# Attention heads: a copy moved from ScalarE to VectorE, low parts to GpSimd, reciprocals of softmax sums taken in pairs

## The chip, the cores and the metric

The kernel runs on one core of one Trainium2 chip. The metric is device time of one execution in microseconds (us); lower is better. Engines are named as in the profile: PE is TensorE (PEld its weight loads), ACT is ScalarE, DVE is VectorE, POOL is GpSimd, SP the queue that issues most DMAs.

## The reference

A two-layer encoder trunk over two independent sequences of 512 tokens, width 1024, in float32: Fourier mixing and an MLP, then attention and an MLP. The change lies in the attention layer: 8 query heads, 2 key/value heads, head size 128.

```python
s = jnp.einsum("bqkgd,bskd->bkgqs", q_blk, k)
p = jax.nn.softmax(s, axis=-1)
o = jnp.einsum("bkgqs,bskd->bqkgd", p.astype(v.dtype), v)
...
return o @ w_o
```

`x_prompt` is sequence 0 and `x_sample` sequence 1; both use the same weights.

## The kernel before, in words

TensorE multiplies in float32r, which holds fewer bits than float32. So nearly every operand is kept as two parts: `hi`, the rounded value (a ScalarE cast, line 86), and `lo`, what is left of it (a VectorE subtraction `src - hi`, line 87). Both stand in the helper `split`. A product is three matmuls: hi by hi, hi by lo, lo by hi (`mm3`, lines 81 to 83). Matmul results lie in PSUM, in tiles `ps` of 128 by 512, of which there are eight.

Attention runs over 16 heads, eight of sequence 0 and then eight of sequence 1. One turn n of the loop handles three heads at once:

1. `scores` for head n, four times, t = 0 to 3 (128 queries each): three matmuls; VectorE takes the row maximum (line 1385); ScalarE the exponential with its row sum (line 1387, tile `p`); VectorE the reciprocal of the sum (line 1388); GpSimd multiplies `p` by it in place (line 1389).
2. `transpose_p` for head n-1, four times, mixed with the scores: four TensorE transposes, one from each of the four finished `p` tiles (line 1395), into one `ps`, then `split` into the operand of step 4. So every group of four transposes reads all four `p` of its head, the last one `p` of t = 3.
3. `transpose_q` for head n+1: four transposes (line 1374) and a `split`.
4. `values` for head n-1: twelve matmuls into one `ps`, `o`. ScalarE copies `o` to SBUF as float32 (line 1412); for sequence 0 alone `split` also makes hi and lo parts from it, which the output projection after the loop reads first (the products `b11` and `b21`, line 820).

In turns 3 to 7 the normalisation of the last query tiles (`norm_rope`, with a square root, lines 136 and 1340 to 1353) runs as a side job, and from turn 7 on the loop also loads and splits projection weights (`load_kept`, tiles `w`), in every second turn. The tiles `p` come from a pool of eight.

In this loop a scheduler puts the instructions of every engine in order, from estimated costs. Every engine then runs its queue strictly in that order, waiting at semaphores.

Of the kernel before, what the change touches and what calls it, by code (L numbers as in the profile page):

```python
# [15 lines left out]
AF = mybir.ActivationFunctionType  # L16
ALU = mybir.AluOpType
# [27 lines left out]
def trunk_kernel(ctx, tc, x_in, xt_in, y_out, tables, rope, gfour, gcol, grow, gfin,  # L45
                 w_four, w_nyq, w_qkv, w_o, w_a22, w_up, w_row2, w_row4, w_sum2, w_sum4, w_down):
    nc = tc.nc
# [13 lines left out]
    def nm(s):  # L61
        n_[0] += 1
        return f"{s}_{n_[0]}"

    def slot(shape, dt):
        return act.tile(shape, dt, tag="u4", name=nm("u"))

    def tm(shape=(P, 512), dt=F32):
        return tmp.tile(list(shape), dt, tag="t2", name=nm("t"))

    def small(n=4):
        return sm.tile([P, n], F32, tag="s", name=nm("s"), padded_shape=[P, 8])

    def ps():
        return psp.tile([P, 512], F32, tag="ps", name=nm("ps"))

    def f32(ap):
        return ap.bitcast(F32)

    def mm3(out, lh, ll, rh, rl, first, last):  # L80
        nc.tensor.matmul(out, lh, rh, start=first, stop=False)  # L81
        nc.tensor.matmul(out, lh, rl, start=False, stop=False)  # L82
        nc.tensor.matmul(out, ll, rh, start=False, stop=last)  # L83

    def split(dst_hi, dst_lo, src, eng=nc.vector):
        nc.scalar.copy(dst_hi, src)  # L86
        eng.tensor_sub(dst_lo, src, f32(dst_hi))  # L87
# [502 lines left out]
    def odd_outs(q, fos):  # L590
        return outs(q, fos, wo, 256, 256)
# [28 lines left out]
    with tc.manual_schedule(engines={ET.PE, ET.Activation, ET.DVE, ET.Pool, ET.SP}):  # L620
# [72 lines left out]
        o = odd_outs(0, range(KC))  # L693
# [596 lines left out]
    for which, sc in (("q", HD ** -0.5), ("k", 1.0)):  # L1290
        r = slot([P, 2, NT, HD], F32)
# [7 lines left out]
    def qkv(cg, q, t, ws, k0=0, k1=KC, o=None):  # L1299
        o = ps() if o is None else o  # L1300
        cols = slice(t * P, (t + 1) * P)
        for k in range(k0, k1):
            w = ws[k // 2]
            c = (k % 2) * 512
            mm3(o, hT[q][k][:, 0, cols], hT[q][k][:, 1, cols],
                w[0][:, c : c + 512], w[1][:, c : c + 512], k == 0, k == KC - 1)
        return o
# [50 lines left out]
    heads_out, ahead = Blocks(None), []  # L1358
# [11 lines left out]
    def transpose_q(q, h):  # L1370
# [5 lines left out]
        split(qT[:, 0], qT[:, 1], pt)  # L1376
        return qT

    def scores(q, h, qT, t):
        kk = kT[q, h // 4]  # L1380
        s = ps()
        cols = slice(t * P, (t + 1) * P)
        mm3(s, qT[:, 0, cols], qT[:, 1, cols], kk[:, 0], kk[:, 1], True, True)
        m, sm_ = small(1), small(1)
        nc.vector.tensor_reduce(m[:, :1], s, AX.X, ALU.max, negate=True)
        p = tm()
        nc.scalar.activation(p, s, AF.Exp, bias=m[:, :1], accum_out=sm_[:, :1])  # L1387
        nc.vector.reciprocal(sm_[:, :1], sm_[:, :1])
        nc.gpsimd.tensor_scalar(p, p, sm_[:, :1], 1.0, ALU.mult, ALU.mult)
        return p  # L1390

    def transpose_p(probs, sc):
# [7 lines left out]
    def values(q, h, pts):  # L1400
        o = ps()
        c = (h // 4) * HD
        for sc in range(NT):
            vh, vl = vt[q][0][:, sc, c : c + HD], vt[q][1][:, sc, c : c + HD]
            mm3(o, vh, vl, pts[sc][:, 0], pts[sc][:, 1], sc == 0, sc == NT - 1)
        i, j = h // 2, h % 2
        name = "b11" if h < 4 else "b21"
        if j == 0:
            heads_out.f[q, i] = slot([P, 2, 512], F32)
            if q == 0:  # L1410
                heads_out.b.setdefault(name, []).append([slot([P, 2, 512], F32R) for _ in range(2)])
        nc.scalar.copy(heads_out.f[q, i][:, j], o)
        if q == 0:
            hi, lo = heads_out.b[name][-1]
            split(hi[:, j], lo[:, j], o)

# [142 lines left out]
    with tc.manual_schedule(engines={ET.Activation}):  # L1561
        o = qkv(1, 1, 2, ws[1])
        probs = [scores(*heads[0], first, t) for t in range(NT)]
        nc.scalar.activation(raw[:, :512], o, AF.Copy, scale=rs[1][:, 2:3])
        qT = transpose_q(*heads[1])
        for _ in turned:
            pass
        o = qkv(1, 1, 3, ws[1])
        nc.scalar.activation(raw[:, 512:], o, AF.Copy, scale=rs[1][:, 3:4])
        head_squares(raw, 0, 4, ss)  # L1570
# [4 lines left out]
    for n in range(1, len(heads) + 1):  # L1575
        pts, nxt = [], []
        for t in range(NT):
            if n < len(heads):
                nxt.append(scores(*heads[n], qT, t))
            pts.append(transpose_p(probs, t))  # L1580
            if n > 2 and t == 0:
                for _ in range(3 if n == 3 else 1):
                    next(todo, None)
        last = nxt[-1] if nxt else last
        if n + 1 < len(heads):
            qT = transpose_q(*heads[n + 1])
        values(*heads[n - 1], pts)
        if n == 2:
            head_squares(raw, 4, 4, ss)
        probs = nxt  # L1590
        if n > 6:
            next(first_rows, None)
# [18 lines left out]
    with tc.manual_schedule(engines={ET.PE}):  # L1611
        o = {}
# [12 lines left out]
        o = {}  # L1625
# [24 lines left out]
        o = {}  # L1650
# [22 lines left out]
    for f in range(2 * PLAIN):  # L1673
        raw = load_raw(plain[f], (P, 2, 512))
        hi, lo = slot([P, 2, 512], F32R), slot([P, 2, 512], F32R)
# [59 lines left out]
    with tc.manual_schedule(engines={ET.PE, ET.Activation, ET.DVE, ET.Pool, ET.SP}):  # L1735
# [17 lines left out]
        x, z = xtok  # L1753
# [3 lines left out]
        def tile(t, c0, c1, at=0, mid=lambda: None):  # L1757
            o = ps()[:, : c1 - c0]
            for k in range(len(ats)):
                ak, wk = ats[k][1], ws[k]  # L1760
                cols = slice(t * P, (t + 1) * P)
                mm3(o, ak[0][:, cols], ak[1][:, cols], wk[0][:, c0:c1], wk[1][:, c0:c1], k == 0, k == len(ats) - 1)
                if k == at:
                    mid()
            return o
# [8 lines left out]
        o = [tile(2, 0, 512, 2, ob.root)]  # L1774
# [6 lines left out]
        o = [tile(3, 0, 512)]  # L1781
# [171 lines left out]
```

## Time and profile before

| what | value |
|---|---|
| time, median of 3 runs | 1691.13 us (1688.81 to 1692.85) |
| span of the profiled execution | 1687.5 us |
| PE busy | 1659.3 us, 98% of the span |
| DVE busy | 1265.4 us, 75% |
| ACT busy | 877.1 us, 52% |
| POOL busy | 382.9 us, 23% |
| granted TensorE clock | 0.999 |
| attention loop in the span | about 853 to 976 us |

The profile gives the span of the profiled execution, from its first to its last instruction, and no other time of that execution. The median of the runs is 3.6 us above the span; what lies around the span is in those 3.6 us. Times in the rows are microseconds from the start of the span; "mean ns" is of one instruction. A row of the timeline starts with its start and its length; instructions that follow each other are pipelined, so a row can overlap the next on the same engine.

### The profile page before, as it was taken

Reading aid. Unit: us, or ns where it says so; the run is one execution under the profiler, and the core shown is the slowest. Engines: PE = TensorE matmul, PEld = TensorE weight load, DVE = VectorE, ACT = ScalarE, POOL = GpSimd, SP = SyncE. Lnnn points to the kernel's source line nnn. Section 1 sums busy time; section 2 is a strip of 40 time slices with the busy share of each in tenths; the row PEclk is TensorE's granted clock in tenths of the full one; section 3 lists DMA queues with packets and bytes.
Section 4 is the critical chain, followed back from the end, with each engine's and each line's share of the span. In section 5 each row is a group of like instructions: output and inputs, shape, how many; then the busy total and the mean of one; then the engine's idle time right before and its main releaser. Section 6 shows DMA issues by size and latency. Waiting matters only on the chain.

```text
span 1687.5 us, 22246 instructions
## 1 busy us (share of the span) xinstructions
PE 1659.3 (98%) x7826; PEld 1382.8 (82%) x7826; DVE 1265.4 (75%) x1867; ACT 877.1 (52%) x1544; POOL 382.9 (23%) x350
## 2 busy tenths in 40 slices
PE   6999999999999999999999999999999999999998
PEld 5988888888888888888878888888888888887887
DVE  8769787456876869868888877787855487878875
ACT  7765445446443435447688855554544553433334
POOL 1320543331000001324544312004422220000002
PEclk9999999999999999999999999999999999999999
DMA  9752555449864757525501146334644696757532
GB/s 309 187 191 85 200 187 189 166 171 338 297 223 152 241 171 240 172 82 171 179 13 38 63 163 224 115 123 156 212 152 157 224 371 200 231 156 231 179 102 100
DMA packets 121808, 302.03 MB, mean 179 GB/s; under 512 B 12361, under 2 KB 13513, under 8 KB 121697
## 3 DMA queue, kind: packets, MB, share of 16 engines
q1 hardware_dynamic: 99184, 255.26, 43.2%
q0 software_dynamic: 8256, 19.40, 5.5%
q10 hardware_dynamic: 14256, 25.96, 4.1%
q8 instruction: 61, 1.00, 0.2%
q14 instruction: 51, 0.41, 0.1%
HBM read 217.15 MB, written 82.38 MB: 177 GB/s over the span
## 4 chain that ended last, share of the span: by engine, by line
PE 84%; DVE 8%; DMA 3%; ACT 3%; issue 2%; SPq 0%; POOL 0%; DVEq 0%; ACTq 0%; POOLq 0%
PE ps L820 67%; PE ps L83 5%; PE ps L81 5%; PE ps L82 5%; DVE u L87 1%; DMA raw<-w_sum 1%; PE ps L1395 1%; DMA u<-x 1%; ACT u L86 1%; DVE w L87 1%; ACT t L1387 1%; DVE u L219 1%; DVE u L1026 1%; DVE u L235 1%; PE ps L172 1%
## 5 line engine op out<-in xcount | busy, mean ns | idle before, releaser
L820 PE MATMUL ps<-u,w 128*128 128x512 f32 x4944 | 1132.0, 390 | 2.4 <-DVE w L87 0.9
L820 PEld LDWEIGHTS ps<-u,w 128*128 128x128 f32 x4944 | 926.8, 188 | 198.1 <-DVE w L87 1.9
L86 ACT CAST w<-raw 128x1024 fp32r<-128x1024 f32 (+1 forms) x216 | 213.8, 995 | 311.2 <-PE ps L820 236.8
L87 DVE TENSOR_TENSOR w<-raw,w 128x1024 fp32r<-128x1024 f32 (+1 forms) x216 | 252.4, 1172 | 77.7 <-ACT w L86 77.4
L86 ACT CAST u<-u 128x1024 fp32r<-128x1024 f32 x144 | 144.7, 1047 | 84.6 <-PE ps L820 35.3
L87 DVE TENSOR_TENSOR u<-u,u 128x1024 fp32r<-128x1024 f32 x144 | 173.3, 1231 | 20.0 <-ACT u L86 19.6
L820 PE MATMUL ps<-u,u 128*128 128x512 f32 x600 | 143.3, 390 | 0.1
L1026 DVE TENSOR_TENSOR u<-ps,u 128x512 f32<-128x512 f32 x160 | 109.7, 687 | 36.7 <-PE ps L820 34.2
L81 PE MATMUL ps<-u,u 128*128 128x512 f32 (+2 forms) x360 | 136.5, 381 | 0.7 <-ACT t L1387 0.3
L936 POOL TENSOR_TENSOR u<-u 128x512 f32<-128x512 f32 x28 | 37.6, 1344 | 427.6 <-ACT u L833 427.6
L1055 POOL DMA_DIRECT2D raw<-w_sum x32 | 27.9, 871 | 469.9 <-DVE w L87 161.6
L83 PE MATMUL ps<-u,u 128*128 128x512 f32 (+2 forms) x360 | 132.3, 368 | 1.1 <-DVE u L87 0.7
L820 PEld LDWEIGHTS ps<-u,u 128*128 128x128 f32 x600 | 112.5, 188 | 24.0 <-ACT u L851 0.5
L82 PE MATMUL ps<-u,u 128*128 128x512 f32 (+2 forms) x360 | 131.6, 366 | 0.3 <-DVE u L87 0.3
L164 POOL TENSOR_TENSOR t<-t,t 128x512 f32<-128x512 f32 (+1 forms) x52 | 74.8, 1443 | 192.1 <-ACT t L160 191.6
L832 ACT ACTIVATE t<-t 128x512 f32<-128x512 f32 x64 | 40.4, 632 | 109.9 <-DVE t L905 99.8
L83 PEld LDWEIGHTS ps<-u,u 128*128 128x128 f32 x360 | 69.7, 194 | 12.2 <-DVE u L87 1.3
L81 PEld LDWEIGHTS ps<-u,u 128*128 128x128 f32 x360 | 69.9, 194 | 10.8 <-ACT u L86 1.8
L87 DVE TENSOR_TENSOR u<-ps,u 128x512 fp32r<-128x512 f32 (+4 forms) x118 | 71.1, 625 | 8.6 <-ACT u L86 8.0
L82 PEld LDWEIGHTS ps<-u,u 128*128 128x128 f32 x360 | 70.0, 195 | 9.1 <-DVE u L87 1.5
L892 DVE TENSOR_TENSOR t<-ps,u 128x512 f32<-128x512 f32 x32 | 22.0, 688 | 61.0 <-PE ps L820 53.2
L86 ACT CAST u<-ps 128x512 fp32r<-128x512 f32 (+4 forms) x118 | 61.1, 546 | 7.4 <-PE ps L1395 4.0
(233 smaller groups left out, 1984.7 us busy)
## 6 DMA issues: line engine op xcount, KB each, us to landing
raw<-w_up SPq DMA_DIRECT2D x80, 512.0 KB, 4.5
u<-spill_t SPq DMA_DIRECT2D x60, 512.0 KB, 7.0
raw<-w_sum SPq DMA_DIRECT2D x56, 512.0 KB, 4.8
u<-spill_b SPq DMA_DIRECT2D x45, 512.0 KB, 6.0
spill_t<-u SPq DMA_DIRECT2D x84, 256.0 KB, 2.0
spill_b<-t ACTq DMA_DIRECT2D x60, 256.0 KB, 4.3
raw<-w_row SPq DMA_DIRECT2D x28, 512.0 KB, 4.6
park<-u SPq DMA_DIRECT2D x24, 512.0 KB, 4.3
```

The costliest lines, as they stand in the source:

```text
L81: nc.tensor.matmul(out, lh, rh, start=first, stop=False)
L82: nc.tensor.matmul(out, lh, rl, start=False, stop=False)
L83: nc.tensor.matmul(out, ll, rh, start=False, stop=last)
L86: nc.scalar.copy(dst_hi, src)
L87: eng.tensor_sub(dst_lo, src, f32(dst_hi))
L164: nc.gpsimd.tensor_add(acc[q][:, :n], acc[q][:, :n], s[:, :n])
L820: nc.tensor.matmul(o, w[x][:, sl], h[k][y], start=first and k + i == 0, stop=k == n - 1 and i == 2, skip_group_check=not first)
L832: nc.scalar.activation(t, src, AF.Relu)
L892: nc.vector.tensor_add(u2, ob, t[:, 0])
L936: eng.tensor_sub(t[:, 0], b12, b11)
L1026: nc.vector.tensor_add(x, o, x)
L1055: nc.gpsimd.dma_start(s[:, 1], w[:, 3], accum_op=ALU.add)
```

## The change

In `scores`, two tiles (t = 0 and 1, t = 2 and 3) share one small tile for their row sums. VectorE takes one reciprocal of both sums after the second tile's exponential, and GpSimd then multiplies both `p` tiles, one after the other. There are 32 reciprocals of two columns where there were 64 of one.

In `values`, sequence 1 is as before. For sequence 0 VectorE copies `o` to SBUF, ScalarE makes the hi part from PSUM, and GpSimd makes the lo part from VectorE's copy and the hi part, both in SBUF. Before, ScalarE made the copy and the hi part, and VectorE the lo part from PSUM.

```diff
+    totals = []
+
     def scores(q, h, qT, t):
...
-        m, sm_ = small(1), small(1)
+        m = small(1)
         nc.vector.tensor_reduce(m[:, :1], s, AX.X, ALU.max, negate=True)
         p = tm()
-        nc.scalar.activation(p, s, AF.Exp, bias=m[:, :1], accum_out=sm_[:, :1])
-        nc.vector.reciprocal(sm_[:, :1], sm_[:, :1])
-        nc.gpsimd.tensor_scalar(p, p, sm_[:, :1], 1.0, ALU.mult, ALU.mult)
+        if t % 2 == 0:
+            totals.append((small(2), p))
+        r, before = totals[-1]
+        nc.scalar.activation(p, s, AF.Exp, bias=m[:, :1], accum_out=r[:, t % 2 : t % 2 + 1])
+        if t % 2:
+            nc.vector.reciprocal(r[:, :2], r[:, :2])
+            for i, x in enumerate((before, p)):
+                nc.gpsimd.tensor_scalar(x, x, r[:, i : i + 1], 1.0, ALU.mult, ALU.mult)
         return p
...
-        nc.scalar.copy(heads_out.f[q, i][:, j], o)
-        if q == 0:
-            hi, lo = heads_out.b[name][-1]
-            split(hi[:, j], lo[:, j], o)
+        if q:
+            nc.scalar.copy(heads_out.f[q, i][:, j], o)
+            return
+        f, (hi, lo) = heads_out.f[q, i], heads_out.b[name][-1]
+        nc.vector.tensor_copy(f[:, j], o)
+        nc.scalar.copy(hi[:, j], o)
+        nc.gpsimd.tensor_sub(lo[:, j], f[:, j], f32(hi[:, j]))
```

The scheduler sees other costs and places other instructions too. In the changed program's order on PE, turns 4 to 9 change: in turns 6 to 9 all four transposes of a group stand together right behind the scores of t = 0, where before the first group stood spread among the scores of t = 0, 1 and 2. The first output products (line 820) move in among the last head's values, and four DMA loads of kept projection weights move ahead of one load of the residual.

## Prediction

> **What bounds the kernel now.** I read the page first (span, engines), then the groups of the attention loop by line, the timeline of PE there, and the timelines of ACT, DVE and POOL in one quiet turn.
>
> ```profile
> span 1687.5 us, 22246 instructions
> PE 1659.3 (98%) x7826; PEld 1382.8 (82%) x7826; DVE 1265.4 (75%) x1867; ACT 877.1 (52%) x1544; POOL 382.9 (23%) x350
> ```
>
> PE is the bound: 98% busy. The change touches only what feeds PE in the attention loop, so it can win what PE loses there, and no more; it can lose as much as it makes PE wait.
>
> ```profile
> 856.65 0.60 PE L1374 MATMUL ps<-ident,u 128*128 128x128 f32 x4
> 872.14 0.60 PE L1374 MATMUL ps<-ident,u 128*128 128x128 f32 x4
> 880.61 0.60 PE L1374 MATMUL ps<-ident,u 128*128 128x128 f32 x4
> 889.55 0.60 PE L1374 MATMUL ps<-ident,u 128*128 128x128 f32 x4
> 944.63 0.60 PE L1374 MATMUL ps<-ident,u 128*128 128x128 f32 x4
> 952.74 0.60 PE L1374 MATMUL ps<-ident,u 128*128 128x128 f32 x4
> 960.47 0.60 PE L1374 MATMUL ps<-ident,u 128*128 128x128 f32 x4
> 971.27 2.23 PE L1395 MATMUL ps<-ident,t 128*128 128x128 f32 x16
> ```
>
> These transposes come once a turn, so they are a clock. The last two rows of L1374 are 7.73 us apart, with PE full: that is a turn's floor. The pair before is 8.11 apart: a turn that also splits projection weights. The worst are 872.14 to 880.61, 8.47, and from there to 889.55, 8.94. From 856.65 to 960.47 are 13 turns in 103.82 us; 13 floors are 100.5. So PE loses 3.3 us in them (2.0 in the two worst, some 0.4 in each of two that split weights, 0.55 elsewhere), and about 0.4 in the last head (sixteen transposes take 2.23 us; at the 0.11 us between transposes in the rows of four they need about 1.85). **3.7 us is all that the change can win in the loop.**
>
> ```profile
> L87 DVE TENSOR_TENSOR u<-ps,u 128x512 fp32r<-128x512 f32 x86 | 57.0, 682 | 5.4 <-ACT u L86 5.0
> L1389 POOL TENSOR_SCALAR t<-t,s 128x512 f32<-128x512 f32 x60 | 43.6, 727 | 67.9 <-DVE s L1388 53.9 <-PE ps L1395 5.6 <-PE ps L83 3.4
> L1395 PE MATMUL ps<-ident,t 128*128 128x128 f32 x256 | 40.0, 274 | 0.3
> L1388 DVE RECIPROCAL s<-s 128x1 f32<-128x1 f32 x60 | 9.4, 157 | 2.2 <-ACT t L1387 1.8
> L1412 ACT COPY u<-ps 128x512 f32<-128x512 f32 x15 | 8.8, 588 | 8.7 <-PE ps L83 8.5
> L164 POOL TENSOR_TENSOR t<-t,t 128x512 f32<-128x512 f32 (+1 forms) x52 | 74.8, 1443 | 192.1 <-ACT t L160 191.6
> ```
>
> Busy time, mean ns and what each waited for. GpSimd waits 53.9 us for reciprocals: it is idle, but what it makes, the scaled `p`, is what PE needs next.
>
> **The chain that decides.** One quiet turn, head 13; its `p` are used from 956.61.
>
> ```profile
> 948.89 0.60 PE L1395 MATMUL ps<-ident,t 128*128 128x128 f32 x4
> 951.16 0.60 PE L1395 MATMUL ps<-ident,t 128*128 128x128 f32 x4
> 952.30 0.60 PE L1395 MATMUL ps<-ident,t 128*128 128x128 f32 x4
> 956.61 0.60 PE L1395 MATMUL ps<-ident,t 128*128 128x128 f32 x4
> 949.52 0.59 ACT L86 CAST u<-ps 128x512 fp32r<-128x512 f32 x1 [0.32 <-PE ps L1395]
> 950.01 0.69 ACT L1387 ACTIVATE t<-ps,s 128x512 f32<-128x512 f32 x1
> 950.68 0.59 ACT L86 CAST u<-ps 128x512 fp32r<-128x512 f32 x1
> 953.46 1.06 ACT L86 CAST u<-ps 128x512 fp32r<-128x512 f32 x2
> 954.40 0.71 ACT L1387 ACTIVATE t<-ps,s 128x512 f32<-128x512 f32 x1
> 956.13 0.59 ACT L1412 COPY u<-ps 128x512 f32<-128x512 f32 x1 [0.92 <-PE ps L83]
> 953.42 0.68 DVE L1385 TENSOR_REDUCE s<-ps 128x1 f32<-128x512 f32 x1
> 955.28 0.15 DVE L1388 RECIPROCAL s<-s 128x1 f32<-128x1 f32 x1
> 954.34 0.70 POOL L1389 TENSOR_SCALAR t<-t,s 128x512 f32<-128x512 f32 x1 [0.72 <-DVE s L1388]
> 955.59 0.69 POOL L1389 TENSOR_SCALAR t<-t,s 128x512 f32<-128x512 f32 x1 [0.55 <-DVE s L1388]
> ```
>
> The last exponential starts at 954.40, its reciprocal at 955.28 (0.88 later), its scaling at 955.59 (0.31 later), done at 956.28. The transposes start at 956.61; the fourth of them, which reads this tile, about 0.33 later (0.60 for four, 0.27 for one). The margin is 0.66 us.
>
> **Pairing the reciprocals.** 32 fewer of 157 ns free 5.0 us of DVE, but in its queue a reciprocal delays what follows by half of that or less, and the one behind the last exponential stays where it is. GpSimd's scaling of t = 2 (at 954.34 now) must wait for 955.28 too, so it starts at 955.59 and that of t = 3 about 0.70 later: done at 956.98, against a need at 956.94. With 0.06 from its end to the transpose,
>
> ```profile
> 893.58 0.69 POOL L1389 TENSOR_SCALAR t<-t,s 128x512 f32<-128x512 f32 x1 [0.56 <-DVE s L1388]
> 894.33 0.33 PE L1395 MATMUL ps<-ident,t 128*128 128x128 f32 x1
> ```
>
> PE waits 0.10. The first pair stands two exponentials and three casts earlier in ACT's queue and is not late. Price: heads 1, 11 and 13, with this order, 0.15 each (0.10 to 0.20): 0.45. Heads 10, 12 and 14 split weights and already run 8.11; their margin is larger:
>
> ```profile
> 947.55 0.70 POOL L1389 TENSOR_SCALAR t<-t,s 128x512 f32<-128x512 f32 x1 [0.28 <-DVE s L1388]
> 946.29 0.98 POOL L1389 TENSOR_SCALAR t<-t,s 128x512 f32<-128x512 f32 x1 [0.72 <-DVE s L1388]
> 946.04 0.67 DVE L87 TENSOR_TENSOR w<-u,w 128x512 fp32r<-128x512 f32 x1
> ```
>
> Done at 948.25 against 949.22, 0.97: the 0.70 fits; 0.05 each, 0.15. Head 15 has no other work in front of its transposes, and they wait for its last tile today (the 0.4 above): the whole 0.70.
>
> **The copy and the order around it.** ACT loses a copy of 588 ns in each of eight heads, 4.7 us; DVE trades a low part of 682 ns for a copy (not in the trace; between ACT's 588 and DVE's 682 from PSUM; I take 682, the same engine). POOL gains eight subtractions; the nearest row with two inputs is 1443 ns, POOL waits most of its time, and their result is read only after the loop. So 4.7 us leave ACT, but are they on the path? In the changed order the hi cast of `o` waits for DVE's copy of the same PSUM tile, and behind that cast wait the next head's first cast and exponential. Values end so that a reader starts at 956.13, 0.48 before the transposes; the copy then ends 0.20 after them, the hi cast starts about 0.27 after and the next cast at 0.74, against 0.63 in head 13 (948.89 to 949.52). ACT waits where it used to copy; the chain starts 0.11 later, not earlier; where the transposes are themselves late by that much, as below, it costs nothing.
>
> The Trainium skill ("PSUM — Partial Sum Buffer", section on bank collisions) says that two engines must not touch one PSUM bank at once, reads included, and that the compiler's scheduler adds a dependency. The row of L87, waiting 5.0 us for L86 on the same tiles, agrees; without that rule the 0.11 would be nothing.
>
> Now the chain in heads 5, 6, 7 and 9 in the changed order, from the first transpose as zero, with head 13's steps: first cast 0.63, exponential 1.12 (0.49 after a cast), cast 1.79 (0.67 after an exponential). Then a second cast stands before exponential 1 and must wait for the third group, 951.16 - 948.89 + 0.63 = 2.90; so exponential 1 is at 3.39, the cast of the fourth group at 4.06 (ready at 952.30 - 948.89 + 0.63 = 4.04), exponential 2 at 4.55, a cast at 5.22, exponential 3 at 5.71, where head 13 has 5.51. DVE adds more: its joint reciprocal of t = 0, 1 stands in front of the third low part and waits for exponential 1 (3.39 + 0.88 = 4.27). Behind it stand a low part, a maximum and two low parts, some 0.6 each (from 953.42 to 955.28 there are three), so the second reciprocal comes at about 6.75 instead of 5.71 + 0.88 = 6.59. With 0.31, 0.70, 0.69 and 0.06 the fourth transpose is at 8.51; PE wants it at 7.72 + 0.33 = 8.05. PE waits 0.46, and has nothing to put there, since the transposes now stand in one block. Heads 2 and 8 have the milder order, 0.30 late by ACT alone. Sum: 4 x 0.46 + 2 x 0.30 = 2.44, less the 0.55 that is lost there today: 1.9. Bounds: 0.5, if DVE's queue runs ahead, and 4, if every late head pays 0.8.
>
> **Heads 3 and 4.**
>
> ```profile
> 870.83 1.28 ACT L136
> 877.29 1.36 POOL L1389 TENSOR_SCALAR t<-t,s 128x512 f32<-128x512 f32 x2 [5.87 <-DVE s L1388]
> ```
>
> Today ACT loads the square root's table, does its side job and loads the exponential's again; POOL gets nothing for 5.87 us, and PE loses 2.0 in two turns. In the changed order one scaling (L1340) instead of three stands before the second load, but then two more and both exponentials precede the last pair: head 3's last tile lands about when it does now, head 4's earlier. I take 0.9 back (0 to 1.5).
>
> **The sum.** 0.45 + 0.15 + 0.70 + 1.9 - 0.9 = 2.3. GpSimd's rows above are quiet ones; its mean is 727, some 0.06 more for a pair in each of 13 heads: 0.8. Together +3.1 us: span 1690.6, and with the 3.6 us that lie between span and median, **1694.2 us**. Bounds of this case: +0.5 and +6. The loads that move on SP hold nothing up: nobody waits for the residual there.
>
> The Trainium skill ("SBUF — State Buffer", section on who interferes with whom) has a GpSimd instruction that reads SBUF and a VectorE instruction with two SBUF inputs block each other. The 0.98 at 946.29, beside a VectorE split with both inputs in SBUF, agrees (0.28 over its neighbours). If each of the eight subtractions met such a wait on the path, the sum would be 8 x 0.28 = 2.2 higher.
>
> ```profile
> 853.00:976.00 123.00, 121.98 (x680) 99.42 (x679) 104.15 (x228) 107.22 (x259) 50.21 (x70) 1.00 0.11 35
> ```
>
> **Rivals.** *Relief* (0.14): ACT and DVE, freed of 4.7 and 5.0 us, run ahead, and exponential 3 comes before 5.4 in all of sequence 0. Then PE's waits go: -3.7 us, 1687.4. For it: both engines are busy for most of the loop (DVE 104.15 and ACT 107.22 of 123 us, third and fourth in the row of the windows above); against it: the chain's waits for PE, not its work, set exponential 3. *Nothing* (0.10): late tiles and recovered turns cancel; 1691.1. The change then does not do what it says: ACT's time was off the path and VectorE's copy too. *Compounding* (0.26): DVE's copy gets stuck behind the late second reciprocal, whose lead on the values' end (7.72 - 0.48 = 7.24) is 7.24 - 6.75 = 0.5 us. Once that is gone, the hi cast and with it the next head's chain start late, so each of eight heads pays another copy of 0.59: +4.7 on the 3.1, 1698.9. *The forecast's own case* has 0.50.
>
> **Chances.** 0.2% is 3.4 us, about what a measurement of this kernel can tell from no change. Of the forecast's 0.50 I put 0.27 above that and 0.23 below; compounding is slower, relief faster, nothing the same: slower 0.53, same 0.33, faster 0.14. Range 1688.5 to 1699.5: the likeliest case's own is 1691.6 to 1697.1; it is widened to compounding's 1698.9 above and most of the way to relief below.
>
> **What would show it.** Turns of heads 5 to 9 at 8.0 to 8.4 us by L1374; PE waiting for L1396 (the new scaling) just before the fourth transpose; scalings of t = 2 and 3 back to back; ACT waiting for DVE before each hi cast of `o`; the last sixteen transposes at 2.8 to 3.0 us. Wrong if turns in sequence 0 stay at 7.7 to 7.8, or if the time outside 853 to 976 moves.

## The result and the profile after

The changed kernel takes 1699.67 us (median of 5 runs, 1698.26 to 1700.60), the kernel before on the same chip 1691.03: a ratio of 1.0053, 95% interval 1.0042 to 1.0063. The forecast was 1694.2 with a range of 1688.5 to 1699.5, whose upper end the median passes by 0.17 us; the direction was right, the size was not: +8.6 us where +3.1 was forecast.

The first lines of the page, profile after:

```profile
span 1698.8 us, 22232 instructions
PE 1663.8 (98%) x7826; PEld 1381.9 (81%) x7826; DVE 1267.1 (75%) x1835; ACT 872.9 (51%) x1536; POOL 393.3 (23%) x358
```

ACT lost 4.2 us of work and POOL gained 10.4; VectorE's total did not fall (1265.4 to 1267.1) although it has 32 instructions fewer. PE has the same matmuls and the program is 11.3 us longer in this execution (8.6 by the medians; the runs of the kernel before lie some 2 us on either side of theirs).

The clock of the attention loop is again the block of transposes of q (L1374). Timeline of PE, kernel after:

```profile
829.50 0.60 PE L1374 MATMUL ps<-ident,u 128*128 128x128 f32 x4
...
867.42 0.60 PE L1374 MATMUL ps<-ident,u 128*128 128x128 f32 x4
875.41 0.60 PE L1374 MATMUL ps<-ident,u 128*128 128x128 f32 x4
885.77 0.60 PE L1374 MATMUL ps<-ident,u 128*128 128x128 f32 x4
894.78 0.60 PE L1374 MATMUL ps<-ident,u 128*128 128x128 f32 x4
903.78 0.60 PE L1374 MATMUL ps<-ident,u 128*128 128x128 f32 x4
...
961.52 0.60 PE L1374 MATMUL ps<-ident,u 128*128 128x128 f32 x4
969.31 0.60 PE L1374 MATMUL ps<-ident,u 128*128 128x128 f32 x4
973.31 0.49 PE L1402 MATMUL ps<-ident,t 128*128 128x128 f32 x3
974.13 0.33 PE L1402 MATMUL ps<-ident,t 128*128 128x128 f32 x1 [0.33 <-POOL t L1396]
...
980.63 0.38 PE L1402 MATMUL ps<-ident,t 128*128 128x128 f32 x2
981.39 2.09 PE L1402 MATMUL ps<-ident,t 128*128 128x128 f32 x14 [0.39 <-POOL t L1396]
```

and the first row of the same stretch before (the prediction shows its last):

```profile
826.65 0.60 PE L1374 MATMUL ps<-ident,u 128*128 128x128 f32 x4
```

Call "the stretch" the time from the first of these blocks to the end of the last transposes of `p`. Before it is 146.85 us (826.65 to 971.27 + 2.23), after 153.98 (829.50 to 981.39 + 2.09): +7.13. A turn is named by the head whose `p` are first transposed in it. By turns:

| turn of head | before | after | more | forecast |
|---|---|---|---|---|
| 1, 11, 13 | 7.76, 7.73, 7.73 | 7.92, 7.86, 7.79 | 0.35 | 0.45 |
| 10, 12 | 8.11, 8.11 | 8.45, 8.46 | 0.7 | 0.10 |
| 2, 6, 7, 8, 9 | 39.07 in all | 40.96 in all | 1.9 | 1.9, with head 5 |
| 3, 4 | 8.47, 8.94 | 10.36, 9.01 | 2.0 | -0.9 |
| 5 | 7.90 | 9.00 | 1.1 | (in the 1.9) |
| 14 and 15, to the end of the stretch | 13.03 | 14.17 | 1.1 | 0.05 and 0.70 |

A further term of the forecast, +0.8 for GpSimd's mean duration, belonged to no one turn. The remaining 1.5 of the 8.6 us lie outside the stretch. Ahead of it both programs have the same instructions. The first block starts 2.85 us later than before in this execution and 1.71 later in another one of the same kernel (below); in the fourteen profiles of this case it starts anywhere from 826.60 to 830.03. So at least a part of the 1.5 changes from one execution to the next.

Who waits for whom, in the stretch of after (engine line waited for: us in total, times, longest us):

```profile
PEld ps L1402 <- POOL t L1396: 8.5, 16, 1.0
ACT u L1424 <- DVE u L1423: 7.3, 6, 1.5
POOL u L1425 <- ACT u L1424: 4.6, 7, 1.7
PE ps L1402 <- POOL t L1396: 4.3, 12, 0.6
```

and in the stretch of before, where PE's matmuls have no such row:

```profile
PEld ps L1395 <- POOL t L1389: 2.4, 8, 0.4
```

After the change PE waits for the scaled `p` in twelve of the sixteen heads (not in 0, 4, 11 and 13): its weight loads 16 times (first row), its matmuls 12 times (last row). ACT waits for VectorE's copy before six of the high parts, and GpSimd's low parts wait for seven high parts.

What happened in head 3, timelines of POOL, DVE, ACT and PE, kernel after:

```profile
879.77 1.37 POOL L1396 TENSOR_SCALAR t<-t,s 128x512 f32<-128x512 f32 x2 [6.28 <-PE ps L83]
881.88 1.29 POOL L1425 TENSOR_TENSOR u<-u,u 128x512 fp32r<-128x512 f32 x1 [0.73 <-ACT u L1424]
883.15 1.51 POOL L1396 TENSOR_SCALAR t<-t,s 128x512 f32<-128x512 f32 x2
881.35 0.17 DVE L1394 RECIPROCAL s<-s 128x2 f32<-128x2 f32 x1
881.21 0.58 ACT L1424 CAST u<-ps 128x512 fp32r<-128x512 f32 x1
883.90 0.55 PE L1402 MATMUL ps<-ident,t 128*128 128x128 f32 x3 [0.54 <-POOL t L1396]
```

The joint reciprocal of t = 2, 3 is there at 881.35; in a quiet turn the scaling follows 0.31 later. Here it starts at 883.15, 1.80 later, since a low part of 1.29 us (of head 2's output) stands in GpSimd's queue between the two pairs, and that one waited first, 0.73, for ScalarE's high part. Nobody needs the low part before the loop ends; PE needs the scaling at once. Before, the same head's last tile was scaled by

```profile
879.04 0.69 POOL L1389 TENSOR_SCALAR t<-t,s 128x512 f32<-128x512 f32 x1 [0.39 <-DVE s L1388]
```

879.73, 7.59 after its turn's first block (872.14); after it is 884.66, 9.25 after its own (875.41).

### The profile page after: what moved, and what is told of

Same layout as the page of the kernel before. It is cut to its first block, busy times and chain, and to the rows that moved or that the text cites. A ratio compares the mean times of both kernels' runs of the same rounds, so it can differ in the third digit from the quotient of the medians.

```text
span 1698.8 us, 22232 instructions
## 1 busy us (share of the span) xinstructions
PE 1663.8 (98%) x7826; PEld 1381.9 (81%) x7826; DVE 1267.1 (75%) x1835; ACT 872.9 (51%) x1536; POOL 393.3 (23%) x358
## 4 chain that ended last, share of the span: by engine, by line
PE 80%; DVE 10%; DMA 4%; issue 2%; ACT 2%; POOL 1%; SPq 0%; DVEq 0%; ACTq 0%; POOLq 0%
PE ps L820 65%; PE ps L82 4%; PE ps L81 4%; PE ps L83 4%; DVE u L87 2%; DMA raw<-w_sum 1%; DVE w L87 1%; POOL t L1396 1%; PE ps L1402 1%; DVE s L1387 1%; DMA u<-spill_t 1%; ACT u L86 1%; DVE u L219 1%; DVE u L1026 1%; PE ps L172 1%
## 5 line engine op out<-in xcount | busy, mean ns | idle before, releaser
L87 DVE TENSOR_TENSOR w<-raw,w 128x1024 fp32r<-128x1024 f32 (+1 forms) x216 | 252.0, 1171 | 77.9 <-ACT w L86 77.6
L87 DVE TENSOR_TENSOR u<-u,u 128x1024 fp32r<-128x1024 f32 x144 | 173.2, 1228 | 20.4 <-ACT u L86 20.0
L87 DVE TENSOR_TENSOR u<-ps,u 128x512 fp32r<-128x512 f32 (+4 forms) x110 | 66.1, 620 | 16.7 <-ACT u L86 15.9
L86 ACT CAST u<-ps 128x512 fp32r<-128x512 f32 (+4 forms) x110 | 57.2, 541 | 14.9 <-PE ps L1402 12.3
```

## The experiments

The theories after the result, which the expectations below name by letter. **A**: the second pair of a head has no slack; scaling t = 3 behind t = 2 makes PE wait 0.1 to 0.5 in every turn. **B**: the low part on GpSimd costs the 3 us of heads 3 to 5, by its place in the queue and by holding up VectorE's small products of the rotary side job. **P**: pairing alone carries all. **C**: the cost is ScalarE's high part waiting for VectorE's copy, which delays the next head's chain (the prediction's compounding rival). **Q**: the load of VectorE's queue sets the chain.

In the table, "time" is the median less that of the kernel before on the same chip, with the interval of the ratio; "stretch" is the profiled stretch less 146.85, which leaves out what varies ahead of the loop; then the turns of heads 3, 4 and 5. "Loop" in the text is the time from the first to the last block of transposes of q (133.82 before, 139.81 after).

An edit also lets the scheduler place other instructions anew. By the order of the traces, e5 has two of PE's some 790 instructions of the stretch elsewhere than after, e12 four, and e8 none elsewhere than e5: these three change little but what their edit says. In the other runs 8 to 93 stand elsewhere than in the kernel with which they are compared, so their small differences by turn may be the order's.

| run | time | ratio, 95% | stretch | turns 3, 4, 5 |
|---|---|---|---|---|
| before | 0 | | 0 | 8.47 8.94 7.90 |
| after | +8.6 | 1.0042-1.0063 | +7.13 | 10.36 9.01 9.00 |
| after, again | +7.7 | 1.0031-1.0056 | +7.13 | 10.37 9.02 8.99 |
| e1 pairs only | +4.5 | 1.0018-1.0038 | +4.48 | 10.26 8.12 7.74 |
| e2 copies only | +1.4 | 0.9997-1.0014 | +0.73 | 9.31 8.71 7.81 |
| e4 first pair only | +1.9 | 1.0002-1.0020 | +0.85 | 10.49 7.77 7.84 |
| e12 first pair, copies | +2.0 | 1.0005-1.0022 | +1.03 | 10.08 8.56 8.47 |
| e5 GpSimd in program order | +5.6 | 1.0020-1.0044 | +5.85 | 9.11 9.07 8.94 |
| e8 low parts later | +3.9 | 1.0014-1.0032 | +3.54 | 9.16 8.79 8.07 |
| e3 low part on VectorE | +5.7 | 1.0018-1.0039 | +3.59 | 9.90 8.25 7.76 |
| e11 t = 3 on VectorE | +5.5 | 1.0024-1.0052 | +4.05 | 10.17 8.80 8.71 |
| e7 t = 1, 3 on VectorE | +10.4 | 1.0054-1.0079 | +9.11 | 10.01 9.04 8.04 |
| e9 single, low parts later | +0.6 | 0.9996-1.0013 | +0.57 | 8.28 8.86 8.24 |
| e10 before, t = 3 on VectorE | -0.3 | 0.9992-1.0011 | -0.15 | 8.53 8.81 8.23 |

**The two parts alone (e1, e2, e4).** e1 takes the paired reciprocals into the kernel before and leaves `values` as it was (against the changed kernel):

```diff
...
-        f, (hi, lo) = heads_out.f[q, i], heads_out.b[name][-1]
-        nc.vector.tensor_copy(f[:, j], o)
-        nc.scalar.copy(hi[:, j], o)
-        nc.gpsimd.tensor_sub(lo[:, j], f[:, j], f32(hi[:, j]))
+        nc.scalar.copy(heads_out.f[q, i][:, j], o)
+        if q == 0:
+            hi, lo = heads_out.b[name][-1]
+            split(hi[:, j], lo[:, j], o)
```

> The kernel before with the paired reciprocals alone; sequence 0's outputs copied and split as before. The loop from the first to the last block of transposes of q takes 133.8 us before and 139.8 after. Theory A+B (pairing makes the last scaling of a head late by 0.1 to 0.7 us; the low part of the outputs on GpSimd, queued between head 3's first and second pair of scalings, makes the turns of heads 3 to 5 late): without the low part those turns give back most of their 3.1 us, the loop is at 136 to 137.5, the last sixteen transposes still start about 0.7 late, the time is 1693.5 to 1696. Rival P (pairing alone carries all): the turns of heads 3 to 5 are at 10.4, 9.0, 9.0 as after, time 1699. Rival C (ScalarE's cast waiting behind VectorE's copy carries the most): the loop is within 1 us of before, time 1691 to 1692.5.

Measured: 1694.66, +4.5 us, loop 137.46, last sixteen transposes late. These are A+B's numbers; P's 1699 and C's 1692.5 both miss. The turns of heads 3 to 5 give back 2.25 of their 3.1, but not as expected: head 3's is 10.26 here too, without any low part on GpSimd, and it is the next two that come back (8.12, 7.74). What makes head 3 late here is seen in e4 below.

e2 is the other half, new copies with a reciprocal for each tile (against the kernel before):

```diff
-        nc.scalar.copy(heads_out.f[q, i][:, j], o)
-        if q == 0:
-            hi, lo = heads_out.b[name][-1]
-            split(hi[:, j], lo[:, j], o)
+        if q:
+            nc.scalar.copy(heads_out.f[q, i][:, j], o)
+            return
+        f, (hi, lo) = heads_out.f[q, i], heads_out.b[name][-1]
+        nc.vector.tensor_copy(f[:, j], o)
+        nc.scalar.copy(hi[:, j], o)
+        nc.gpsimd.tensor_sub(lo[:, j], f[:, j], f32(hi[:, j]))
```

> The kernel before with the new copies alone (copy by VectorE, high part by ScalarE, low part by GpSimd from the copy); one reciprocal for each tile as before. In GpSimd's queue the low part then stands between the third and the fourth scaling of heads 3 and later. Theory A+B: no pair is late, but the fourth scaling waits behind a low part of 1.29 us that itself waits for ScalarE, in up to six heads: loop 135.5 to 138.5, time 1692.5 to 1696. Rival P: the loop is within 1 us of before, 1691 to 1692. Rival C: loop 138 to 140, time 1696 to 1699, with ScalarE's waits for VectorE's copy at 1 us each or more.

Measured: 1691.59, +1.4 with an interval that reaches zero; loop 134.54. That is P's number for this run, below the range for A+B and far from C's 1696 to 1699: by themselves the copies cost little or nothing. The low part stood in front of a last scaling in head 3 only, not in six heads as expected.

e4 pairs t = 0, 1 and leaves t = 2, 3 single, with `values` as in e1 (against the changed kernel):

```diff
+        if t > 1:
+            r = small(1)
+            nc.scalar.activation(p, s, AF.Exp, bias=m[:, :1], accum_out=r[:, :1])
+            nc.vector.reciprocal(r[:, :1], r[:, :1])
+            nc.gpsimd.tensor_scalar(p, p, r[:, :1], 1.0, ALU.mult, ALU.mult)
+            return p
```

> The kernel before, with one reciprocal for the tiles t = 0 and 1 of a head and one each for t = 2 and 3; outputs copied and split as before. Theory A (the first pair has slack, the second none): the fourth transpose of a head comes as before, the last sixteen transposes too; loop 133.5 to 134.5, time 1690.5 to 1692. Rival P (any pairing costs): half of what the run with both pairs loses.

Measured: 1692.10, loop 134.52, each a hair above A's range; stretch +0.85. P's half of what both pairs lose (2.2) would fit the median, not the stretch (0.85 of 4.48). The second pair carries the other 3.63.

But the first pair is not free, as A and the prediction have it: its 0.85 lie in heads 3 and 4 (18.26 for the two turns, 17.41 before). Timelines of ACT and POOL, kernel before:

```profile
869.50 0.75 ACT L1387 ACTIVATE t<-ps,s 128x512 f32<-128x512 f32 x1
874.85 1.28 ACT L1387 ACT_TABLE_LOAD   x1
876.15 0.69 ACT L1387 ACTIVATE t<-ps,s 128x512 f32<-128x512 f32 x1
870.73 0.69 POOL L1389 TENSOR_SCALAR t<-t,s 128x512 f32<-128x512 f32 x1 [2.52 <-DVE s L135]
```

and of POOL and PE, e4 (line 1402 is the pair's scaling there, line 1408 the transpose):

```profile
877.29 1.36 POOL L1402 TENSOR_SCALAR t<-t,s 128x512 f32<-128x512 f32 x2 [9.15 <-DVE s L1400]
878.03 0.33 PE L1408 MATMUL ps<-ident,t 128*128 128x128 f32 x1 [1.27 <-POOL t L1402]
```

Head 3's exponentials of t = 0 (869.50) and t = 1 (876.15) stand on either side of ScalarE's square root job and its two table loads. Before, t = 0 was scaled at once, at 870.73. Joined to t = 1 it is scaled at 877.29, with ScalarE's instructions around it in the same order, and PE's first transpose waits 1.27 us for it. e1 has the same wait of 1.27, the changed kernel one of 0.59 (at 880.52). In e4 head 4's turn is then 1.17 shorter than before, so that the two together lose 0.85.

The parts add up to 4.48 + 0.73 = 5.21, and the change costs 7.13. 1.9 us come only from having both.

**The changed kernel again.** No edit.

> The changed kernel itself once more, unaltered, on the chip on which the next three run. The profiled execution of the first time has 2.85 us more than before already ahead of the attention loop, where both programs have the same instructions, and loads landed later. If that is chance of loads, this time's start of the loop lies anywhere from 826.6 to 829.5, while the loop itself is again 139.8 (0.3 either way); the median then is 1697 to 1699.7. If it belongs to the program, the loop starts at 829 again.

Measured: 1697.84 against 1690.19. The stretch is the same to 0.01 us; its first and last rows, timeline of PE:

```profile
828.36 0.60 PE L1374 MATMUL ps<-ident,u 128*128 128x128 f32 x4
...
980.25 2.09 PE L1402 MATMUL ps<-ident,t 128*128 128x128 f32 x14 [0.38 <-POOL t L1396]
```

828.36 to 982.34 is 153.98. So the stretch's +7.13 belongs to the program, and 1.14 of the first execution's 2.85 ahead of it do not. The median, 1697.84, is 1.83 below the first one and inside the forecast's range. That is why the stretch, not the median, is read below for differences under 2 us.

**The low part's place (e5).** GpSimd's instructions of the loop are held in the order of the program, which puts every low part behind the four scalings:

```diff
-    for n in range(1, len(heads) + 1):
+    with tc.manual_schedule(engines={ET.Pool}):
+        for n in range(1, len(heads) + 1):
```

> The changed kernel with GpSimd's instructions of the attention loop held in the order in which the program issues them, so that head 3's low part stands behind its four scalings and not between the pairs; nothing else is altered. Theory B: head 3's second pair starts about 0.3 us after its reciprocal instead of 1.8, the turns of heads 3 to 5 (10.4, 9.0, 9.0 after; 8.5, 8.9, 7.9 before) give back 1.5 to 3 us; the other turns stay; time 1696.5 to 1698.2. Rival P (the pair alone makes them late): those turns stay, time 1699.5. Rival C: the same, 1699.5.

Measured: 1695.77, 0.7 below B's range; the stretch is 1.28 shorter than after, nearly all in head 3's turn (10.36 to 9.11). Timelines of POOL and DVE, e5:

```profile
878.10 1.36 POOL L1396 TENSOR_SCALAR t<-t,s 128x512 f32<-128x512 f32 x2 [6.27 <-PE ps L83]
880.02 1.36 POOL L1396 TENSOR_SCALAR t<-t,s 128x512 f32<-128x512 f32 x2 [0.56 <-DVE s L1394]
881.34 1.29 POOL L1425 TENSOR_TENSOR u<-u,u 128x512 fp32r<-128x512 f32 x1
879.68 0.17 DVE L1394 RECIPROCAL s<-s 128x2 f32<-128x2 f32 x1
```

The second pair follows its reciprocal by 0.34 and ends at 881.38, 7.65 after the turn's first block (873.73): where the kernel before has it (7.59). Turns 4 and 5 stay at 9.07 and 8.94. B is right on the place, with a little less in these turns (1.25) than its 1.5 to 3; P and C foresaw no change here. That head 3 still takes 0.64 more than before fits the first pair, whose first transpose waits 0.59 here too (at 878.85).

**The low part beside VectorE (e8, e3).** e8 is e5 with the eight low parts put off to sequence 1's heads, one or two a head:

```diff
...
+            for _ in range(1 if h else 2):
+                if lows:
+                    lows.pop(0)()
...
-        nc.gpsimd.tensor_sub(lo[:, j], f[:, j], f32(hi[:, j]))
+        lows.append(lambda: nc.gpsimd.tensor_sub(lo[:, j], f[:, j], f32(hi[:, j])))
```

> The changed kernel with GpSimd in program order (as in the run before, 1695.8), and its eight low parts put off to the turns of sequence 1's heads; VectorE still copies and ScalarE still casts the outputs. Theory B (the low part on GpSimd in the same turns as VectorE's small products of the rotary side job stretches these: 0.28 us one without it, up to 1.4 beside it): those products are at 0.28 to 0.45 again, the turns of heads 3 to 5 (9.1, 9.1, 8.9 with GpSimd in order) give back 1 to 1.5 us, loop 137 to 137.6, time 1693.8 to 1695. Rival C (VectorE's copy in front of ScalarE's cast carries what the copies cost): those turns stay, time 1695.8.

Measured: 1694.11, loop 136.53; the stretch is 2.30 shorter than e5's. The turns of heads 4 and 5 give back 0.28 and 0.87, as B has it; most of the rest comes from heads 2, 7 and 8 and from the last two. ACT still waits for VectorE's copy as long as in after (7.3 us there), by the waits of e8:

```profile
ACT u L1427 <- DVE u L1426: 7.4, 6, 1.5
```

With that wait whole, the kernel is cheaper than the one with pairs alone (3.54 against 4.48), and e9 (below) has 7.3 us of it at a cost of 0.57. So C has fallen: the wait is there and costs nothing that shows.

What the low part does to VectorE's products is seen in the timelines of POOL and DVE, kernel after:

```profile
892.74 1.28 POOL L1425 TENSOR_TENSOR u<-u,u 128x512 fp32r<-128x512 f32 x1 [1.71 <-ACT u L1424]
892.81 1.56 DVE L1351 TENSOR_TENSOR t<-u,u 128x128 f32<-128x128 f32 x2
```

A product of 128x128 starts 0.07 after GpSimd's subtraction, and the two of them end at 894.37, 0.35 after the subtraction does (894.02): the first was held until the subtraction was through. Behind them in VectorE's queue stand a maximum and the low parts of the next chain. All eight products, by the groups of DVE from 870 to 912 us (busy us, mean ns), in before:

```profile
L1351 DVE TENSOR_TENSOR t<-u,u 128x128 f32<-128x128 f32 x8 | 2.2, 300 | 0.0
```

in after:

```profile
L1351 DVE TENSOR_TENSOR t<-u,u 128x128 f32<-128x128 f32 x8 | 4.3, 557 | 0.0
```

in e5:

```profile
L1351 DVE TENSOR_TENSOR t<-u,u 128x128 f32<-128x128 f32 x8 | 5.3, 678 | 0.0
```

and in e8:

```profile
L1351 DVE TENSOR_TENSOR t<-u,u 128x128 f32<-128x128 f32 x8 | 3.0, 394 | 0.0
```

so after loses 2.1 us there, e5 3.1 and e8 0.8. Not all of that is the low part's. In after one product alone meets it, the one at 892.81 (1.36 instead of 0.28); the others that are stretched, to 0.57 to 0.75, meet GpSimd's scaling or the side job's own product on GpSimd (line 1348), and so do those of e8.

What the held product costs is seen in head 5's turn. The two products that stand in a row about the end of head 4's turn take 0.47 to 0.48 together in before, e1, e3, e4, e8 and e10, and head 5's turn is 7.74 to 8.23 there; 0.78 to 0.98 in e2, e7 and e9, with 7.81 to 8.24; and 1.52 to 1.56 in e5, e11, e12 and after, with 8.47 to 9.00.

e3 gives the low part to VectorE instead:

```diff
-        nc.gpsimd.tensor_sub(lo[:, j], f[:, j], f32(hi[:, j]))
+        nc.vector.tensor_sub(lo[:, j], o, f32(hi[:, j]))
```

> The changed kernel with the low part of the outputs by VectorE from PSUM instead of GpSimd; VectorE has the copy as well, so it does 8 times 0.68 us more than before the change. Theory B: without a low part on GpSimd the products are at 0.28 to 0.45 and nothing stands between head 3's pairs but 1.5 us of VectorE's queue more in each head of sequence 0: loop 138 to 140, time 1695.5 to 1698. Rival C (a queue on VectorE is what costs): slower than the changed kernel, 1700 to 1703.

Measured: 1695.84, in B's range, with a loop of 136.28 that is below it (this loop starts at 830.03, the latest of all). The products are at 0.32, and C's 1700 to 1703 is far off. Eight instructions of 0.69 more on VectorE cost less here (stretch +3.59) than eight of 1.3 on GpSimd (+7.13).

**Low part without a second pair (e12).** After, with t = 2 and 3 single by the same edit as e4's.

> The changed kernel with single reciprocals for t = 2 and 3; the first pair stays, and so do the new copies with GpSimd's low part, which stands in front of head 3's last scaling. If the two parts of the change add up, the loop and last head cost 0.85 (first pair alone) plus 0.73 (copies alone): loop 135.3 to 135.8, time 1692 to 1693. If the low part costs what it does (3.6 us of 7.1) only because a pair waits behind it, the same; if it costs that by itself, 1694.5 or more.

Measured: 1692.27, loop 135.0, stretch +1.03: no more than the sum of e4 and e2 (1.58). Here too VectorE's products are stretched (0.52 in the mean by the same group; the one beside the low part again takes 1.36). It is not free where it stands: heads 4 and 5 are 0.79 and 0.63 longer than in e4. But other turns are shorter by nearly as much (the stretch is 0.18 longer than e4's). Against after, this run gives back 6.10 us by taking the second pair apart; without the copies that pair costs 3.63 (e1 less e4). So the low part is dear mainly together with a second pair. That the pair takes the slack that hid the rest is a reading of these numbers; no run measures the slack.

**The second pair itself (e7, e11).** e7 gives the second scaling of every pair to VectorE:

```diff
-            for i, x in enumerate((before, p)):
-                nc.gpsimd.tensor_scalar(x, x, r[:, i : i + 1], 1.0, ALU.mult, ALU.mult)
+            for i, x, e in ((0, before, nc.gpsimd), (1, p, nc.vector)):
+                e.tensor_scalar(x, x, r[:, i : i + 1], 1.0, ALU.mult, ALU.mult)
```

> The changed kernel with the second scaling of each pair on VectorE, so that the two tiles of a pair are scaled side by side. Theory A (the last tile is late because it is scaled behind its partner on GpSimd, 0.70 us or 1.1 beside a split of weights): the fourth transpose of a head comes without a wait in heads 6 to 14 again, their turns lose the 0.06 to 0.48 that the change put on each (2.5 us in all) and the last head its 0.8 or so; head 3's low part still stands between its pairs. Loop 137 to 138, time 1694.5 to 1696.5. Rival Q (the thirty scalings load VectorE's queue, which is what sets the chain): those turns stay above 8.1 and the time is 1698 or more.

Measured: +10.4, stretch +9.11, the slowest of all; the turns of heads 6 to 13 are at 8.3 to 8.8. These are Q's numbers. The edit loads VectorE's queue with 18.3 us, by the groups of DVE from 853 to 980 us:

```profile
L1396 DVE TENSOR_SCALAR t<-t,s 128x512 f32<-128x512 f32 x29 | 18.3, 630 | 0.1
```

so it moves two things at once, and A is not refuted by it. e11 is the narrower one, t = 3 alone:

```diff
-                nc.gpsimd.tensor_scalar(x, x, r[:, i : i + 1], 1.0, ALU.mult, ALU.mult)
+                (nc.vector if i and t == NT - 1 else nc.gpsimd).tensor_scalar(x, x, r[:, i : i + 1], 1.0, ALU.mult, ALU.mult)
```

> The changed kernel with only the last tile of each head (t = 3) scaled by VectorE, right behind the second joint reciprocal; t = 0, 1, 2 stay with GpSimd. VectorE takes 15 scalings (0.49 us each in the run that did the same to the kernel before, at no cost there) where the run that took 29 lost 1.4 us of loop. Theory A (the last tile is late because it is scaled behind its partner): the turns of heads 6 to 14 give back most of the 2.6 us that they gained, the last head 0.5 to 1.1; the turns of heads 3 to 5 keep what the low part costs them. Loop 137 to 138, time 1694 to 1696. Rival Q (the second tile of the pair is not what is late; VectorE's queue is): turns of heads 6 to 14 as after, time 1697 to 1700.

Measured: 1695.73, loop 137.67, both in A's range; the stretch is 3.08 shorter than after. The turns of heads 1, 2 and 10 to 13 are at 7.73, 7.76, 8.18, 7.73, 7.90 and 7.72, within 0.1 of before or under it, and the last two heads give back 0.94 of 1.14. But heads 7 and 9 are no better (8.60, 8.22). So A holds where nothing but the pair is late, in sequence 1 above all; in the middle heads something else sets the turn, VectorE's queue by Q, which no run here separates.

**Versions that might beat both (e9, e10).** e9 is before with the new copies, the low parts put off and GpSimd held in program order as in e8:

```diff
...
-        nc.scalar.copy(heads_out.f[q, i][:, j], o)
+        nc.vector.tensor_copy(f[:, j], o)
+        nc.scalar.copy(hi[:, j], o)
+        lows.append(lambda: nc.gpsimd.tensor_sub(lo[:, j], f[:, j], f32(hi[:, j])))
```

> The kernel before (one reciprocal for each tile) with outputs of sequence 0 copied by VectorE, cast by ScalarE, and their low parts put off to sequence 1's turns on GpSimd, in program order. No pair, no low part beside the rotary products: theory A+B has nothing left that costs, and VectorE and ScalarE are each freed of work in sequence 0: loop 132.5 to 134, time 1688.5 to 1690.5 (before: 1690.2 to 1691). Rival C (the cast waiting for VectorE's copy delays the next head's chain): loop 135 to 136, time 1691.5 to 1692.5.

Measured: +0.6, no difference from before that the measurement can tell; the loop, 134.39, lies between the two ranges. ScalarE has 4.7 us less to do (872.4 us on its page, 877.1 before), and nothing is won. VectorE is not freed, other than the expectation says: it makes a copy of 0.69 in place of each subtraction of 0.68 (1267.9 us, 1265.4 before).

e10 is before, with only the scaling of t = 3 moved to VectorE:

```diff
-        nc.gpsimd.tensor_scalar(p, p, sm_[:, :1], 1.0, ALU.mult, ALU.mult)
+        (nc.vector if t == NT - 1 else nc.gpsimd).tensor_scalar(p, p, sm_[:, :1], 1.0, ALU.mult, ALU.mult)
```

> The kernel before with only the last tile of each head (t = 3) scaled by VectorE, behind its reciprocal, instead of GpSimd; nothing of the change. Theory A says that what stands between the last reciprocal and the transposes (0.31 to GpSimd's start and 0.70 of scaling) is the margin of a head; half a us less of it gives back what the turns lose today: last sixteen transposes at 2.0 instead of 2.23, head 3's and 4's turns by some tenths; loop 132.8 to 133.8, time 1688.5 to 1690.5 (before: 1690.2). Rival Q (VectorE's queue sets the chain): slower, 1691 to 1693.

Measured: -0.3, again none. The last sixteen transposes take 1.91 instead of 2.23, as expected, and the turn of head 5 loses it again (8.23 against 7.90). No version beat the kernel before.

## Why the prediction was wrong in size, point by point

**What held.** PE bound, little to win and much to lose. The second pair back to back, PE waiting for L1396 just before the fourth transpose (974.13 above), heads 1, 11 and 13 at 0.35 (0.45 forecast; in 11 and 13 the profile shows no wait of PE for a scaling, so there the reason is not shown), the last sixteen transposes at 2.85 (980.63 to 983.48) where 2.8 to 3.0 was named, 0.62 more than before (0.70 forecast). Heads 2, 6, 7 and 9 came out at 7.99, 8.14, 8.22 and 8.13, where the floor of 7.73 and the forecast's waits of 0.30 (heads 2 and 8) and 0.46 give 8.03 and 8.19; head 8, at 8.48, did not. e11 takes the scaling behind its partner away and leaves heads 7 and 9 no shorter, so in these the pair is not the only thing that is late, which is what the forecast's chain says. ACT's wait for VectorE's copy was foreseen, and the sentence that it "costs nothing" where the transposes are late is what e8 shows. The row of L87 that the prediction takes as a sign of such waits shows something else: line 87 subtracts the high part that line 86 makes, and has to wait for it in any case. The sign is the row of L1424 and L1423 above.

**The step that failed: heads 3 and 4, -0.9 forecast, +2.0 measured.** The text says "head 3's last tile lands about when it does now". By e5 that would be so, 7.65 after the turn's start against 7.59; in the changed kernel it is 9.25, because the new low part is queued in between. The mistake stands one paragraph earlier: "POOL waits most of its time, and their result is read only after the loop". The eight subtractions were costed at nothing on GpSimd's idle time. The question was not how idle GpSimd is but what stands behind each subtraction in its queue and what that subtraction waits for; the order of GpSimd's queue in the changed program would have shown it. This is worth 1.2 of the 2.9 us missed: with the low part behind the pairs (e5) the two turns take 18.18 instead of 19.37.

The second mistake in the same step is the sentence "The first pair stands two exponentials and three casts earlier in ACT's queue and is not late". In head 3 the square root job stands between its two exponentials, and PE waits for t = 0. That is about 0.8: e5's 18.18 against 17.41 before, and 18.26 in e4, which has the first pair alone. The last 0.9 is what the forecast took back. Of the runs only e9 and e10, without pairs, come below the 17.41 of before, with 17.14 and 17.34.

The low parts' further cost, 2.30 over all heads (e5 to e8), was in no term either.

**Head 5**, 0.46 forecast, 1.1 measured: the low part beside VectorE's product; its turn is 0.87 shorter in e8 than in e5.

**Heads 10, 12 and 14**, 0.05 each forecast, 0.34, 0.35 and 0.5 measured. The prediction read their margin of 0.97 as holding a scaling of 0.70. Timelines of after, head 10:

```profile
939.69 1.89 POOL L1396 TENSOR_SCALAR t<-t,s 128x512 f32<-128x512 f32 x2 [1.38 <-DVE s L1394]
940.33 0.68 DVE L87 TENSOR_TENSOR w<-u,w 128x512 fp32r<-128x512 f32 x1
941.63 0.33 PE L1402 MATMUL ps<-ident,t 128*128 128x128 f32 x1 [0.32 <-POOL t L1396]
```

The pair takes 1.89 instead of 1.37: moved back by the pairing, the last scaling now runs beside VectorE's split of a weight, which it did not before. The 0.98 for such a meeting was in the prediction's own rows, but was not put on the last tile. The term of 0.8 for GpSimd's longer mean was meant for such meetings, and spread evenly; all of it and more fell on the three heads where there was no cover for it.

**The rivals.** Compounding came nearest in its number (1698.9) and is wrong in its mechanism: it puts 0.59 on each of eight heads by the copy's wait, and e8 and e9 keep the copies and the wait at +3.54 with pairs, +0.57 without. Relief is wrong: the change frees ScalarE of 4.2 us and PE's waits grow; e9 frees it of 4.7, without a pair, and gains nothing. The forecast also said that it would be wrong if the time outside 853 to 976 moved; by the medians less the stretch it moved by 1.5 the first time and by 0.5 the second, which is no more than two executions of one kernel differ by. One figure of what the prediction says can be won is off by little: sixteen transposes at 0.11 need 1.92, not 1.85, and e10 shows 1.91.

**VectorE and GpSimd holding each other.** The product at 892.81 took 1.36 us instead of 0.28, until the subtraction of 1.28 beside it was through. This is the rule that the prediction cites from the Trainium skill's page "SBUF — State Buffer" (section on who interferes with whom), and the trace agrees. The prediction priced it at 2.2 us "if each of the eight subtractions met such a wait on the path" and left it out of the sum. In after one of the eight held a product up; e5 to e8 give 2.30 for all that the low parts cost beyond their place, so the two numbers lie near each other by chance. In e12 a product is held as long, and the run costs no more than the sum of its parts (1.03 against 1.58): a delay is not a price.

**What stays open.** Some 1.9 us are only there with both parts. e5 shows what the low part's place costs, and e8 that the low parts cost 2.30 more in sequence 0, 1.15 of it in heads 4 and 5; how the rest runs, in heads 2, 7 and 8 and the last two, is not shown, nor what sets the turns of heads 7 and 9.

## What to carry to other kernels

A step moved to an idle engine is free only if nothing urgent is queued behind it and what it waits for comes early; read the new order of that engine's queue, not its busy share. Joining two small operations saves their fixed cost and makes the earlier one wait for the later one's input; look at what stands between the two inputs in the queue of the engine that makes them (here, once, two table loads). Where the joined work ends just before it is needed, delays elsewhere cost more than they did before (6.10 us for the second pair with the low parts, 3.63 without). For effects under 0.2%, compare a stretch between two fixed instructions across profiles: here it repeated to 0.01 us in two executions whose medians lay 1.8 apart.

## What the runs showed of the hardware

Answers by line for after (least, median and most ns of GpSimd's subtraction, of its scaling and of VectorE's copy):

```profile
L1425 POOL TENSOR_TENSOR u<-u,u x8: 1281/1292/1646, 864.3 to 925.7; 128x512 fp32r<-128x512 f32 x8
L1396 POOL TENSOR_SCALAR t<-t,s x64: 693/697/1216, 850.2 to 981.3; 128x512 f32<-128x512 f32 x64
L1423 DVE COPY u<-ps x8: 679/692/693, 862.9 to 924.3; 128x512 f32<-128x512 f32 x8
```

and the group of VectorE's scaling from 853 to 980 us in e10:

```profile
L1389 DVE TENSOR_SCALAR t<-t,s 128x512 f32<-128x512 f32 x15 | 7.4, 494 | 0.6
```

GpSimd's subtraction of two 128x512 tiles takes 1.29 us, nearly twice its scaling of one (0.70). A VectorE product with both inputs in SBUF that started 0.07 us after it was held to its end (0.28 became 1.36 at 892.81), and GpSimd's scaling in its turn grew to 1.2 beside a VectorE subtraction with both inputs in SBUF (the second of the two at 939.69). One scaling took 0.49 on VectorE in e10, and 0.63 in the mean in e7. A table load on ScalarE took 1.28 (874.85 before). VectorE's copy of a tile from PSUM, 0.69, lasts as long as its subtraction from it (682 ns in the prediction's row of L87), so the trade of the one for the other freed nothing on VectorE.
